# Early splits of v's first units and weights, residual loads inside an issue_after block, and gathered rows added one step after their fetch

## The chip, the cores and the metric

The kernel runs on one core of one Trainium2 chip. A core has five engines with queues of their own: TensorE (PE, with its weight loads as PEld), VectorE (DVE), ScalarE (ACT), GpSimd (POOL) and SyncE (SP), which here issues most of the DMAs. The metric is device microseconds (us) of one execution; of several runs the median counts.

## The reference

One decoder layer over 256 tokens of width 2048, in float32. What matters here is its last part, the PEER layer, and the two layer norms around it:

```python
h = layer_norm(ALPHA * x + mix, ln1_g, ln1_b)
y = layer_norm(ALPHA * h + peer_ffn(h), ln2_g, ln2_b)

def peer_ffn(xc):                      # 256 tokens, 8 heads, 16 experts a head
    ...                                # two top-16 searches give expert (16384) and gate
    u_sel = u[expert]; v_sel = v[expert]
    act = gelu(einsum('td,thkd->thk', xc, u_sel))
    return einsum('thk,thkd->td', gate * act, v_sel)
```

Each token uses 128 of the 16384 experts. An expert is a pair of rows, one of `u` and one of `v`, each of 2048 elements.

## The kernel before

**How the PEER layer is cut up.** An expert's number is `i1 * 128 + i2`. For 1408 of the 2048 columns of `u`, and for 1536 of those of `v`, the kernel doesn't gather: it runs through all 16384 experts densely, in 128 steps (one for each `i2`) of 128 experts (all `i1`). The remaining 640 columns of `u` and 512 of `v` (`GU`, `GV`) are gathered, row by row, with 256 indirect DMAs each (128 rows of a slot, for each of 128 slots and two tiles of 128 tokens).

**The stages.** After the first layer norm and the search come three stages. The *u stage* writes, for every step, the products of all tokens with 128 rows of `u` to S, a tile of 64 parts (two steps a part) in SBUF. The *extraction* (`extract`, `scatter`, 32 blocks of 8 tokens) picks each token's 128 products out of S with one-hot matrices (`at`, `bt`, `a_hot`), applies gelu and gate, and scatters the weights back into S (`aw`, `wps`). The *value stage* then runs 128 steps; a step reads its weights from S (`weights`, 128 experts by 256 tokens) and multiplies them with three units of `v` (128 by 512 each), summing in PSUM in six banks `vacc`. The last four steps run in a tail of their own from copies (`last`), followed by the residual sum, the second layer norm and the stores.

**Split float32.** A float32 operand is multiplied as two float32r halves: ScalarE casts `hi` (line 94), VectorE subtracts and gives `lo` (line 95), and each product is three matmuls, lines 119 to 121. So each step needs three `hi`, three `lo`, a `hi` and a `lo` of the weights, and 18 matmuls. There are four buffers each for `hi` and `lo`, in the pool `stream`. In the extraction the same buffers (tags `hi` and `lo`) hold `at` and `bt` of the blocks with `b % 4 < 2`; the others use four tags each of the pool `big`, alternating between even and odd blocks.

**Loads.** `load_unit` loads a unit of `v` to a `raw` tile (four buffers), or takes a part of S that has been read already and was filled ahead (`v_place`, `v_follow`, `v_unit`); 23 units, all in the first 13 steps, use `raw`, the other 361 use S. From step 13 on the plan fills 3.5 parts a step, and so runs further and further ahead of use. The loads are issued by SP.

**Gathers.** `add_gathered` takes a step's share of the 256 gathers (`spread`, steps 0 to `GVE` = 120), issues them on GpSimd (`v_gather`, line 805), and adds them with VectorE to `accg`, weighted (line 813). The buffers are three of tag `g`, and from step `LEND` on also the four of `raw`.

**Residual.** `residual` (eight calls, written behind steps 32 to 46) loads the normalized input from DRAM (`pre`) and a slice of gain and bias (`g1`, one buffer; it appears as `g<-ln`), and applies them on GpSimd (lines 827, 828).

**What sets the order.** The kernel is written with a tile framework. At compile time it puts the instructions of each engine into an order, by their place in the program, by priority (`tc.high_priority(offset=AHEAD)` moves an instruction 3000 places forward) and by its own estimate of when buffers and operands are ready; on the chip each queue then runs in that order. A tile of a tag waits until the tag's earlier tile in the same buffer has been released. `with tc.issue_after(ins)` adds an edge, of order alone, from `ins` to each instruction of the block that is on the engine of `ins`. `last_split[0]` is the VectorE instruction of the latest split. The last instructions of the extraction are copies into S by VectorE (line 748).

## Time and profile before

| | |
|---|---|
| median of 3 runs | 1747.99 us |
| the runs | 1747.92, 1747.99, 1755.24 us |
| the profiled execution's own time | 1756.99 us |
| its span, first to last instruction | 1755.2 us |
| TensorE's busy time | 1666.4 us (95%), mean granted clock 0.984 |
| VectorE | 1450.0 us (83%) |
| ScalarE, GpSimd | 897.5 us (51%), 886.7 us (51%) |
| DMA | 451.13 MB, mean 257 GB/s |

The profile is of one execution. Its lines name the engine, the line of the kernel, the operation and the tiles (`out<-in`); a bracket gives the idle time of the engine before an instruction and what ended it. Matmuls are pipelined, and a busy TensorE is not TensorE at its peak; its granted clock is given as a share of 2.4 GHz (1.00 is 2.4 GHz, 0.50 is 1.2 GHz, between them a mean over a stretch). In the trace the extraction takes from about 1011 to 1176 us, the value stage from there to about 1739 us.

### The profile page before, as it was taken

Reading aid. Unit: us, or ns where it says so; the run is one execution under the profiler, and the core shown is the slowest. Engines: PE = TensorE matmul, PEld = TensorE weight load, DVE = VectorE, ACT = ScalarE, POOL = GpSimd, SP = SyncE. Lnnn points to the kernel's source line nnn. Section 1 sums busy time; section 2 is a strip of 40 time slices with the busy share of each in tenths; the row PEclk is TensorE's granted clock in tenths of the full one; section 3 lists DMA queues with packets and bytes.
Section 4 is the critical chain, followed back from the end, with each engine's and each line's share of the span. In section 5 each row is a group of like instructions: output and inputs, shape, how many; then the busy total and the mean of one; then the engine's idle time right before and its main releaser. Section 6 shows DMA issues by size and latency. Waiting matters only on the chain. (4 is left out here: it accounts for less than half of the span.)

```text
span 1755.2 us, 33099 instructions
## 1 busy us (share of the span) xinstructions
PE 1666.4 (95%) x10652; PEld 1484.7 (85%) x10652; DVE 1450.0 (83%) x3515; ACT 897.5 (51%) x1885; POOL 886.7 (51%) x899
## 2 busy tenths in 40 slices
PE   8999999989899999999999889988999999999996
PEld 8999888869888999999999788876687888888883
DVE  6766676679999888889888798877888888889896
ACT  6545565444344555555554358773454555555551
POOL 0000000036775656566565588856747645456562
PEclk9999999989999999999999999998999999999998
DMA  7667657726688999999999841137999999999962
GB/s 219 179 188 192 203 175 261 255 79 214 193 287 268 337 361 321 323 347 336 344 330 329 293 146 55 55 103 255 296 329 333 381 338 332 338 319 328 352 200 89
DMA packets 206014, 451.13 MB, mean 257 GB/s; under 512 B 26928, under 2 KB 31472, under 8 KB 205328
## 3 DMA queue, kind: packets, MB, share of 16 engines
q1 hardware_dynamic: 164816, 297.93, 51.4%
q0 software_dynamic: 41024, 151.09, 24.7%
q8 instruction: 84, 1.38, 0.3%
q14 instruction: 90, 0.74, 0.1%
HBM read 444.59 MB, written 4.26 MB: 256 GB/s over the span
## 5 line engine op out<-in xcount | busy, mean ns | idle before, releaser
L94 ACT CAST hi<-S 128x512 fp32r<-128x512 f32 x677 | 420.4, 622 | 450.5 <-PE vacc L121 223.2
L95 DVE TENSOR_TENSOR lo<-S,hi 128x512 fp32r<-128x512 f32 x672 | 464.5, 701 | 89.6 <-ACT hi L94 81.4
L121 PE MATMUL ups<-hTh,lo 128*128 128x256 f32 x1408 | 392.2, 283 | 11.7 <-DVE lo L95 11.1
L119 PE MATMUL ups<-hTh,hi 128*128 128x256 f32 x1408 | 392.2, 280 | 4.5 <-ACT hi L94 4.2
L120 PE MATMUL ups<-hTl,hi 128*128 128x256 f32 x1408 | 394.0, 281 | 0.0
L659 POOL DMA_INDIRECT g<-u_g,e_idx x256 | 289.2, 1130 | 173.1 <-DVE g L684 119.4
L94 ACT CAST hi<-raw 128x512 fp32r<-128x512 f32 x327 | 202.0, 621 | 245.4 <-PE projT L120 58.9
L95 DVE TENSOR_TENSOR lo<-raw,hi 128x512 fp32r<-128x512 f32 x303 | 216.6, 720 | 111.3 <-ACT hi L94 107.2
L120 PE MATMUL vacc<-lo,wt 128*128 128x512 f32 x744 | 278.4, 401 | 8.6 <-DVE lo L95 8.5
L121 PEld LDWEIGHTS ups<-hTh,lo 128*128 128x128 f32 x1408 | 263.5, 189 | 16.8 <-DVE lo L95 15.6
L121 PE MATMUL vacc<-hi,wt 128*128 128x512 f32 x744 | 276.2, 399 | 0.0
L119 PEld LDWEIGHTS ups<-hTh,hi 128*128 128x128 f32 x1408 | 266.0, 189 | 6.1 <-ACT hi L94 6.1
L120 PEld LDWEIGHTS ups<-hTl,hi 128*128 128x128 f32 x1408 | 265.7, 189 | 0.0
L119 PE MATMUL vacc<-hi,wt 128*128 128x512 f32 x744 | 231.2, 400 | 7.3 <-ACT wt L94 6.9
L805 POOL DMA_INDIRECT g<-v_g,e_idx x139 | 166.3, 1196 | 128.4 <-DVE accg L813 109.0
L684 DVE SCALAR_TENSOR_TENSOR g<-g,h_gath 128x640 f32<-128x640 f32 x256 | 204.9, 820 | 16.6 <-DMA g<-u_g,e_idx 16.1
L805 POOL DMA_INDIRECT raw<-v_g,e_idx x117 | 137.2, 1173 | 84.7 <-DVE accg L813 65.2
L120 PEld LDWEIGHTS vacc<-lo,wt 128*128 128x128 f32 x744 | 141.1, 190 | 45.7 <-DVE lo L95 12.0
L119 PEld LDWEIGHTS vacc<-hi,wt 128*128 128x128 f32 x744 | 141.2, 190 | 42.9 <-ACT wt L94 8.0
L121 PEld LDWEIGHTS vacc<-hi,wt 128*128 128x128 f32 x744 | 140.9, 189 | 34.5 <-issue 0.5
L714 POOL TENSOR_SCALAR bt<-cst,slotT 128x128 f32<-128x128 f32 x192 | 126.3, 675 | 23.3 <-POOL bt L714 16.4
L294 POOL TENSOR_TENSOR bias<-bias,score 128x128 f32<-128x128 f32 (+1 forms) x16 | 11.5, 739 | 233.1 <-DMA bias<-relb 115.8
(243 smaller groups left out, 3074.1 us busy)
## 6 DMA issues: line engine op xcount, KB each, us to landing
S<-v_d SPq DMA_DIRECT2D x361, 256.0 KB, 5.1
S<-u_d SPq DMA_DIRECT2D x328, 256.0 KB, 5.3
raw<-w_t SPq DMA_DIRECT2D x100, 256.0 KB, 2.8
raw<-w_n SPq DMA_DIRECT2D x64, 256.0 KB, 2.8
raw<-w_o SPq DMA_DIRECT2D x64, 256.0 KB, 3.3
raw<-w_q SPq DMA_DIRECT2D x48, 256.0 KB, 3.1
bc<-i_dram SPq DMA_DIRECT2D x32, 256.0 KB, 3.1
raw<-u_d SPq DMA_DIRECT2D x24, 256.0 KB, 5.1
```

The costliest lines, as they stand in the source:

```text
L94: last_copy[0] = nc.scalar.copy(hi, src).ins
L95: last_split[0] = (eng or nc.vector).tensor_tensor(lo, src, hi.bitcast(F32), op=ALU.subtract).ins
L119: mm(o, l[0], r[0], start=first, stop=False)
L120: mm(o, l[0], r[1], start=False, stop=False)
L121: return mm(o, l[1], r[0], start=False, stop=last).ins
L294: nc.gpsimd.tensor_tensor(bias[:, tt, :n], bias[:, tt, :n], sel[:, tt, :n], op=ALU.add)
L659: nc.gpsimd.indirect_dma_start(out=g, out_offset=None, in_=table, in_offset=bass.IndirectOffsetOnAxis(ap=e_idx[:, tt, slot:slot + 1], axis=0))
L684: nc.vector.scalar_tensor_tensor(g, g, 1.0, h_gath[:, tt], op0=ALU.mult, op1=ALU.mult, accum_out=pd[:, tt, slot:slot + 1])
L714: eng.tensor_scalar(bt[j][:, i], iota, i2T[:, t:t + 1], None, op0=ALU.is_equal)
L805: nc.gpsimd.indirect_dma_start(out=g, out_offset=None, in_=A["v_g"], in_offset=bass.IndirectOffsetOnAxis(ap=e_idx[:, tt, slot:slot + 1], a ...
```

## The change

- `VE` = 4 units of `v` are loaded and split at block 28 of the extraction (`v_early`), the first half of the step-0 weights is split after block 16 and the second half after the last block, into two tiles `wt0` of their own; the value stage takes them from there. For that, blocks from `T // EB - VB` = 28 on keep `at` and `bt` in `big`, and the `stream` buffers are left to the units.
- The body of `residual` stands in `with tc.issue_after(last_split[0])`.
- `add_gathered` issues the gathers of its step, but adds those that were issued in the step before; one more call behind the last step takes what is left. Gathers are spread over steps `GV0` = 10 to `GVE` = 123 (before: 0 to 120), and use the `raw` buffers from step 10 on (before: 24).

```diff
--- before.py
+++ after.py
@@ -58,9 +58,12 @@
 LEAD = 5
 LAG = 1
 KEEP0 = 40
-LEND = 24
+LEND = 10
 GL = 4
-GVE = 120
+GV0 = 10
+GVE = 123
+VE = 4
+VB = 4
 ED = 2
 EA = 2
 TAIL_POOL = ((0, 1, 2), (0,))
@@ -695,7 +698,7 @@
     hot_tags = ("h5", "l5")
 
     def halves(name, tags, b, sname):
-        if b % 4 >= 2:
+        if b % 4 >= 2 or b >= T // EB - VB:
             return [big.tile([P, EB // 2, P], F32, name=name, tag=tags[b % 2 * 2 + i]) for i in range(2)]
         return [stream.tile([P, EB // 2, P], F32, name=name, tag=sname, bufs=4) for i in range(2)]
 
@@ -748,10 +751,22 @@
                 put(S[:, :, t // 2].rearrange("p a c j -> p j a c"),
                     wps[:, (i % 4 - 1) * P:(i % 4 + 1) * P].rearrange("p (j a c) -> p j a c", j=2, c=2))
 
+    def split_weights(wt, i2, sl):
+        split(paired(wt[0][:, sl]), paired(wt[1][:, sl]), step_of(i2, sl))
+
+
+    tokens = [slice(tt * P, (tt + 1) * P) for tt in range(NT)]
+    wt0 = [wqp.tile([P, T], F32R, name=f"wt0{s}", tag=f"subk{s}") for s in "hl"]
+    v_early = []
     ahead = extract(0)
     for b in range(T // EB):
         here, ahead = ahead, extract(b + 1) if b + 1 < T // EB else None
         scatter(b, *here)
+        if b == T // EB // 2:
+            split_weights(wt0, 0, tokens[0])
+        if b == T // EB - VB:
+            v_early = [load_unit(A["v_d"][n]) for n in range(VE)]
+    split_weights(wt0, 0, tokens[1])
     for tt in range(NT):
         tp = bankB("wTp")[:, :P]
         nc.tensor.transpose(tp, wT[:, tt * P:(tt + 1) * P], ident)
@@ -762,11 +777,10 @@
     acc = [[(bankA, bankB)[tt]("vacc") for c in range(NC)] for tt in range(NT)]
     accg = big.tile([P, NT, GV], F32, name="accg", tag="h1")
     nc.vector.memset(accg, 0.0)
-    def weights(i2, tts):
+    def weights(i2):
         pair = big.tile([P, 2, T], F32R, name="wt", tag=("l1", "h2")[i2 % 2])
         wt = [pair[:, n] for n in range(2)]
-        for sl in tts:
-            split(paired(wt[0][:, sl]), paired(wt[1][:, sl]), step_of(i2, sl))
+        split_weights(wt, i2, slice(0, T))
         return wt
 
     def product(wt, tt, c, w, i2):
@@ -806,10 +820,14 @@
                                      in_offset=bass.IndirectOffsetOnAxis(ap=e_idx[:, tt, slot:slot + 1], axis=0))
         return g
 
+    fetched = []
+
     def add_gathered(i2):
+
         with tc.issue_after(last_split[0]):
-            for tt, slot in spread(i2, 0, GVE):
-                g = v_gather(i2, tt, slot)
+            due = fetched[:]
+            fetched[:] = [(tt, slot, v_gather(i2, tt, slot)) for tt, slot in spread(i2, GV0, GVE)]
+            for tt, slot, g in due:
                 nc.vector.scalar_tensor_tensor(accg[:, tt], g, pd[:, tt, slot:slot + 1], accg[:, tt],
                                                op0=ALU.mult, op1=ALU.add)
 
@@ -819,26 +837,27 @@
     def residual(c, hf):
         g1 = small.tile([P, 2, T], F32, name="g1", tag="h_gath")
         sl = slice(c * 512 + hf * T, c * 512 + (hf + 1) * T)
-        for i in range(2):
-            nc.sync.dma_start(g1[:, i], A["ln1"][i:i + 1, sl].broadcast_to([P, T]))
-        for tt in range(NT):
-            o = pre[tt][c][:, hf * T:(hf + 1) * T]
-            nc.sync.dma_start(o, z_dram[tt][:, sl])
-            nc.gpsimd.tensor_tensor(o, o, g1[:, 0], op=ALU.mult)
-            nc.gpsimd.tensor_tensor(o, o, g1[:, 1], op=ALU.add)
+        with tc.issue_after(last_split[0]):
+            for i in range(2):
+                nc.sync.dma_start(g1[:, i], A["ln1"][i:i + 1, sl].broadcast_to([P, T]))
+            for tt in range(NT):
+                o = pre[tt][c][:, hf * T:(hf + 1) * T]
+                nc.sync.dma_start(o, z_dram[tt][:, sl])
+                nc.gpsimd.tensor_tensor(o, o, g1[:, 0], op=ALU.mult)
+                nc.gpsimd.tensor_tensor(o, o, g1[:, 1], op=ALU.add)
 
     def finish(tt, c, lo, hi, src):
         o = pre[tt][c][:, lo:hi]
         nc.vector.scalar_tensor_tensor(o, o, ALPHA, src, op0=ALU.mult, op1=ALU.add)
 
-    tokens = [slice(tt * P, (tt + 1) * P) for tt in range(NT)]
     count[0] = 0
     for i2 in range(P - GL):
-        wt = weights(i2, tokens if i2 == 0 else [slice(0, T)])
+        wt = weights(i2) if i2 else wt0
         units = []
         for c in range(NC):
             raw = v_unit(i2, c)
-            units.append(load_unit(A["v_d"][i2 * NC + c], raw))
+            m = i2 * NC + c
+            units.append(v_early[m] if m < VE else load_unit(A["v_d"][m], raw))
             if i2:
                 for tt in range(NT):
                     product(wt, tt, c, units[c], i2)
@@ -847,6 +866,8 @@
                 for c in range(NC):
                     product(wt, tt, c, units[c], 0)
         add_gathered(i2)
+        if i2 == P - GL - 1:
+            add_gathered(P)
         if 32 <= i2 < 48 and i2 % 2 == 0:
             residual((i2 - 32) // 4, (i2 - 32) // 2 % 2)
     last = [big.tile([P, 2, T], F32, name="last", tag="l2"), small.tile([P, 2, T], F32, name="last", tag="h_gath")]
```

## Rows read from the trace of the kernel before

**Rows 1.** Windows of 42 us, all engines: busy us (instructions), clock, DMA share, GB/s.
```profile
1176.00:1218.00 42.00, 33.48 (x126) 25.37 (x127) 28.64 (x38) 16.01 (x33) 24.39 (x26) 0.88 0.74 240
...
1386.00:1428.00 42.00, 42.00 (x182) 33.81 (x181) 35.74 (x59) 21.62 (x40) 21.52 (x20) 1.00 0.99 353
```

**Rows 2.** Windows of the value sums' matmuls alone, same columns without ACT and POOL.
```profile
1192.00:1200.00 8.00, 7.42 (x26) 5.99 (x27) 0.00 (x0) 0.78 0.76 239
1208.00:1216.00 8.00, 5.97 (x18) 4.39 (x19) 0.00 (x0) 0.79 0.79 259
1240.00:1248.00 8.00, 7.65 (x27) 6.17 (x28) 0.00 (x0) 0.79 0.85 250
1342.00:1346.00 4.00, 3.62 (x9) 2.91 (x10) 0.00 (x0) 0.57 0.99 337
1358.00:1716.20 358.20, 358.20 (x1537) 288.38 (x1536) 0.00 (x0) 1.00 0.93 322
```

**Rows 3.** Timeline of TensorE, 1172 to 1350 us: start, length, [idle before <-releaser].
```profile
1192.58 1.22 PE L119 MATMUL vacc<-hi,wt 128*128 128x512 f32 x2 [5.87 <-ACT wt L94]
...
1212.03 0.50 PE L120 MATMUL vacc<-lo,wt 128*128 128x512 f32 x1 [2.03 <-DVE lo L95]
...
1240.35 0.80 PE L120 MATMUL vacc<-lo,wt 128*128 128x512 f32 x1 [3.14 <-DVE lo L95]
...
1342.38 0.79 PE L120 MATMUL vacc<-lo,wt 128*128 128x512 f32 x1 [2.52 <-DVE lo L95]
```

**Rows 4.** Timeline of VectorE, 1176 to 1250 us.
```profile
1237.08 2.62 DVE L813 SCALAR_TENSOR_TENSOR accg<-g,pd,accg 128x512 f32<-128x512 f32 x1 [3.12 <-DMA g<-v_g,e_idx]
```

**Rows 5.** Timeline of ScalarE and of SP's queue, 1176 to 1250 us.
```profile
1191.59 0.62 ACT L94 CAST hi<-raw 128x512 fp32r<-128x512 f32 x1 [7.68 <-DMA raw<-v_d]
...
1184.60 0.81 SPq L823 DMA_DIRECT2D g<-ln  x2
...
1185.51 8.36 SPq L104 DMA_DIRECT2D raw<-v_d  x5
```

**Rows 6.** Timeline of GpSimd, 1020 to 1250 us.
```profile
1130.77 1.12 POOL L805 DMA_INDIRECT g<-v_g,e_idx  x1 [0.15 <-issue]
...
1183.51 1.06 POOL L828 TENSOR_TENSOR pre<-pre,g 128x256 f32<-128x256 f32 x1
```

**Rows 7.** Timeline of GpSimd, TensorE and VectorE in the extraction.
```profile
1108.31 3.76 POOL L714 TENSOR_SCALAR bt<-cst,slotT 128x128 f32<-128x128 f32 x6 [0.83 <-POOL bt L714]
...
1112.00 1.05 PE L745 MATMUL wps<-bt,aw 128*128 128x128 f32 x8
...
1173.39 0.75 DVE L813 SCALAR_TENSOR_TENSOR accg<-g,pd,accg 128x512 f32<-128x512 f32 x1 [0.23 <-ACT pd L758]
```

**Rows 8.** Groups by form, 1176 to 1260, then 1400 to 1700 us (mean ns).
```profile
L813 DVE SCALAR_TENSOR_TENSOR accg<-g,pd,accg 128x512 f32<-128x512 f32 x22 | 21.7, 992 | 11.1 <-DMA g<-v_g,e_idx 11.1
...
L95 DVE TENSOR_TENSOR lo<-S,hi 128x512 fp32r<-128x512 f32 x26 | 22.8, 900 | 1.4 <-ACT hi L94 1.4
...
L813 DVE SCALAR_TENSOR_TENSOR accg<-raw,pd,accg 128x512 f32<-128x512 f32 x83 | 61.4, 744 | 0.0
...
L95 DVE TENSOR_TENSOR lo<-S,hi 128x512 fp32r<-128x512 f32 x214 | 146.7, 689 | 41.1 <-ACT hi L94 37.9 <-DMA S<-v_d 1.7
```

**Rows 9.** Windows of line 813, the additions, on VectorE.
```profile
1386.00:1428.00 42.00, 14.13 (x19) 1.00 0.99 353
...
1680.00:1722.00 42.00, 21.70 (x30) 1.00 0.55 157
```

**Rows 10.** Timeline of GpSimd and VectorE, late in the value stage.
```profile
1334.90 0.95 POOL L805 DMA_INDIRECT g<-v_g,e_idx  x1 [0.30 <-issue]
...
1722.62 0.73 DVE L813 SCALAR_TENSOR_TENSOR accg<-raw,pd,accg 128x512 f32<-128x512 f32 x1
...
1740.48 0.26 DVE L434 BATCH_NORM_AGGREGATE mv<-stats 128x2 f32<-128x24 f32 x1
```

**Rows 11.** Window of the value stage with its highest DMA rate, all engines.
```profile
1360.00:1380.00 20.00, 20.00 (x88) 16.09 (x87) 17.77 (x31) 10.57 (x20) 15.94 (x13) 1.00 1.04 387
```

## The prediction

> **What bounds the kernel now.** I went from the windows of the value stage to TensorE's own timeline in it, then to the engines that it waited for, then back to the extraction that comes before it. From about 1358 us to the end of the step loop at 1716.2 us TensorE is the bound and nothing else: 1537 matmuls in 358.2 us, 0.2331 us each, so 18 matmuls or 4.2 us a step, at a granted clock of 1.00 (2.4 GHz) and with no idle time [rows 1, 2]. There is nothing to win there. The first 40 steps are another matter. The first ten steps' worth of time holds 126 matmuls where a settled stretch of the same length holds 182 [rows 1], and the reader sees why in four gaps of TensorE [rows 3]: 5.87 us before 1192.58 and 2.03, 3.14 and 2.52 us before 1212.03, 1240.35 and 1342.38. Behind each gap the granted clock is below 1.00 for a while: 0.78, 0.79, 0.79 and 0.57, a mean over stretches at 1.2 and at 2.4 GHz [rows 2]. Busy time by the share of clock missing gives what that costs: 7.42 x 0.22 = 1.6, 5.97 x 0.21 = 1.25, 7.65 x 0.21 = 1.6, 3.62 x 0.43 = 1.55 us.
>
> Three of the gaps have one cause. In each, VectorE stands in front of an addition of a gathered row that hasn't landed (2.08, 3.12 and 3.10 us; the middle one is shown [rows 4]), and the `lo` halves of the next units, which TensorE waits for, are queued behind it on VectorE. With the clock: 2.03 + 1.25 + 3.14 + 1.6 + 2.52 + 1.55 = 12.1 us. The first gap is a transfer: ScalarE waits 7.68 us for a raw unit [rows 5]. SP issued it at 1185.51, right behind a pair of residual loads (`g<-ln`) issued at 1184.60, which had to wait until GpSimd had finished with the first residual (its last operation starts at 1183.51 and takes 1.06 us [rows 6]). 5.87 + 1.6 = 7.5 us.
>
> **The additions.** Moved to the step after the fetch, an addition has one step, 4.2 us, more between issue and use; the waits above were 2.08 to 3.12 us, so each is covered. Before step 11 there are no additions at all, and two of the three gaps lie there or just behind, in the time with three gather buffers. From step 10 gathers have seven, as they had from step 24. I take the whole 12.1 us off. Bounds: 12.1, and 7 if one of the three only moves to another place.
>
> **The residual loads.** `issue_after` ties an instruction to the given one only if both are on the same engine. `last_split` is a VectorE instruction; `residual` issues DMAs on SP and operations on GpSimd, none on VectorE. So I read this edit as empty. The trace has the same helper at work: in `add_gathered(0)` the gather stands in the same kind of block, behind the split of step 0, and yet GpSimd issues a gather at 1130.77 us [rows 6], in the midst of the extraction, far ahead of that step's splits. The 16 `pre` loads, 16 `g1` loads and 32 GpSimd operations therefore stay where the order of SP and GpSimd put them, right behind the extraction. What changes around them: units 0 to 3 are split in the extraction, so the raw loads of units 4 to 7 leave SP before the residual loads, and no gather stands beside them on the DMA queues for ten steps. The raw load of unit 9 can still end up behind the second pair of `g1`. Bounds 0 and 7.5 us off; half, 3.7 us, is what I take.
>
> **The early units.** The four units' splits leave the last stretch of the extraction, and so do two additions (0.75 us, the first at 1173.39 [rows 7]), which now lie between the last copies into S on VectorE; together some 2.5 us of VectorE's time (two additions and two `lo` of 0.69 us [rows 8], less some overlap). Against it: the last four blocks now take their `at` and `bt` from `big` alone, so a block's `bt` must wait until the block two before has been scattered. Today GpSimd starts a block's `bt` at 1108.31 us while the matmuls that read the `bt` of two blocks earlier run until 1112.00 + 1.05 = 1113.05 [rows 7]. That is up to 4.7 us for the whole tile and 2.6 us for its first half, which ends at about 1110.9; once for blocks 28 and 29 and perhaps again for 30 and 31. Bounds: 2.5 us off, 5.4 us on. I take 1 us off, since later blocks lose waits of other queues when they start later. The split of the first half of the step-0 weights is one small instruction on ScalarE and one on VectorE, a quarter of a unit's size; both engines have free time in the middle of the extraction, and I cost it at nothing (uncovered, under 1 us by the 0.69 us of a whole `lo`).
>
> **The gathers' end.** 256 gathers now have 113 steps, not 120: 2.27 a step where it was 2.13. VectorE pays 0.74 us for each [rows 8] and is busy 35.74 of 42 us [rows 1], so the time is there. Not so clear is the pace. Between 1386 and 1554 us four stretches of 42 us, ten steps, held 19 additions each (one is shown), though rows were behind: the last is added at 1722.62 us, 23 us after its step 119 ends by 4.2 us a step. In the last stretch it was 30, when most unit loads were done (DMA share 0.55) [rows 9, 10]. If the pace is midway between 1.9 and 2.27 a step for the 104 steps until then, and 3 a step in the last 8, 217 + 24 = 241 are done by the last step; 15 are left, and GpSimd issues one in 0.95 + 0.30 = 1.25 us [rows 10]: 19 us. Now the last addition starts 6.4 us behind the loop. The span ends 39 us behind the loop, of which about 24 must follow the last addition (14.7 us from the second aggregate at 1740.48 [rows 10] to the end, some 9 for the first tile of tokens), so 15 us are hidden. 0 to 4 us on; I take 1.
>
> **The sum.** The profiled execution's own time is 1756.99 us: 1755.2 us span and 1.8 us around it. 1757.0 - 12.1 - 3.7 - 1 + 1 = 1741.2 us. The median of the runs shown is 9.0 us lower than that execution, and one of the three runs lies 7.3 us above the other two, which is about the size of the first gap with its clock. So part of the gaps is probably not in the median runs; then 1741.2 stands as it is. If the 9 us lie elsewhere, the same gain leads to 1732.2. I take 3 of the 9 off: 1738 us, 0.57% under the median.
>
> **Two rules against it.** The operations of GpSimd that belong to the residual lengthen VectorE's: an addition takes 992 ns in the mean between 1176 and 1260 us, beside them, and 744 ns without them [rows 8]. The Trainium skill (SBUF — State Buffer, SBUF: two separate sides) says that a VectorE operation with two SBUF inputs and a GpSimd operation that reads SBUF take turns on one port pair; the trace agrees. It matters if the pin does hold (the third rival). And the Trainium skill (DMA: Bandwidth & Descriptors, Specifications) puts a core's share of HBM at about 358 GB/s; this trace moves 387 GB/s between 1360 and 1380 us, and TensorE loses nothing [rows 11], so the measurement decides. By the page's figure the estimate would be a shortage: 3.5 units and 2.27 gathers a step, 256 KB each, are 1.51 MB in 4.2 us, 360 GB/s.
>
> **Rivals.** *The first gap stays whole* (0.22). SP's order stays as it is and unit 9 comes behind `g1`: 1757.0 - 12.1 = 1744.9, or 1735.9 with the other reading of the median. For it: the empty pin. Against it: the raw units before it are out of the way. *The two-deep tiles stretch the extraction* (0.10): 1741.2 + 1 + 5.4 = 1747.6. For it: the 1108.31 against 1113.05; against it: one block's latency may shrink. *The pin holds* (0.05): the first gap goes whole, and 32 GpSimd operations fall into steps 32 to 46. Between 1176 and 1260 us, beside them, an addition took 0.25 us more and a `lo` 0.21 us more [rows 8]; for 22 additions and 45 `lo` that is 15 us of VectorE's time, and in the 63 us of those steps it has 9.4 us free. 5.5 us short and 1.6 for the clock: 1741.2 - 3.8 + 7.1 = 1744.5. *Slower: the gathers come late* (0.08). At 1.9 a step all through, 215 are done and 41 left at the last step, 51 us; behind the last addition still come those 24 us. The loop would end near 1700, so 1700 + 51 + 24 + 1.8 = 1777. It gets slower by over 0.5% when more than about 25 rows are left, that is at under 2.04 a step. For it: four windows at 1.9. Against it: 30 in the last. *Better: both kinds of gap go and the 9 us lie elsewhere* (0.05): 1757 - 12.1 - 7.5 - 9 = 1728.
>
> **How the numbers follow.** The forecast (0.50) covers 1732 to 1742 us. The 8 in 10 go from 1729 (nearly all of the better case is below) to 1749 (the first two rivals and the pin are inside; the late gathers and a little more are above). 0.5%, 8.7 us, is about what the measurement can tell from no change: faster means under 1739.2. Of the forecast 0.42 lies below that, of the first rival 0.06, and the better case 0.05: 0.53. Slower is the late gathers, 0.08. The remaining 0.39 is the same.
>
> **What would show it.** In the profile after: no additions before step 11, no wait of VectorE for a gather over 1 us, and granted clock 1.00 from about step 4 on; `pre<-z_dram` on SP still right behind the extraction (else the pin holds); the gap of TensorE at unit 9 at 0 to 6 us; the last `bt` of GpSimd no later than 1160 us or so (else the tiles); the last addition within 15 us of the loop's end (else the gathers). The prediction is wrong if a new wait of over 5 us stands in the loop, or if the loop's first steps lose their matmuls to a cause not named here.

## The result: slower by 0.9%

The changed kernel takes 1767.25 us (median of 5 runs, 1765.21 to 1770.31) against 1750.62 us for the kernel before (median of 5, 1747.92 to 1755.24): a ratio of 1.0092, 95% interval 1.0072 to 1.0112. The forecast was 1738 us, with 1729 to 1749 as its range.

The profiled execution of after takes 1765.21 us, with a span of 1763.4 us where before had 1755.2. The span falls into three parts. The loop is counted from its first matmul behind the extraction's last one (a few of step 0 run earlier, between those of the extraction); it starts at 1175.22 us (before 1176.19): 1.0 us earlier. From there to the first matmul of the last four steps it is 534.9 us (before 540.2): 5.3 us less. From that matmul to the end it is 53.3 us (before 38.8): 14.5 us more. -1.0 - 5.3 + 14.5 = +8.2 us. The medians lie 16.6 us apart; the other 8.4 us are the profiled executions' places among the runs (before's is 6.4 us above its median and slower than all five of its runs, after's 2.0 below), and no pair of rows shows what they are. So the 5.3 us by which the loop got shorter may be less, or nothing, between the medians.

The same windows of 42 us of after, all engines, columns as in [rows 1]:

```profile
1176.00:1218.00 42.00, 36.10 (x145) 27.77 (x143) 19.81 (x29) 15.29 (x30) 17.60 (x22) 0.96 0.62 182
1218.00:1260.00 42.00, 37.06 (x140) 29.27 (x141) 27.85 (x47) 19.16 (x37) 25.16 (x26) 0.88 0.82 263
1386.00:1428.00 42.00, 42.00 (x182) 33.81 (x181) 35.46 (x59) 21.96 (x40) 22.70 (x20) 1.00 0.96 340
```

The first ten steps' worth of time holds 145 matmuls now instead of 126, and VectorE does 29 instructions instead of 38 (the additions don't begin before 1237.9). But the next 42 us hold only 140. The timeline of TensorE says why; columns as in [rows 3]:

```profile
1188.62 1.12 PE L122 MATMUL vacc<-hi,wt 128*128 128x512 f32 x2 [2.65 <-ACT wt L97]
...
1197.34 0.73 PE L122 MATMUL vacc<-hi,wt 128*128 128x512 f32 x2 [1.31 <-ACT hi L97]
...
1219.58 1.22 PE L122 MATMUL vacc<-hi,wt 128*128 128x512 f32 x2 [3.51 <-ACT hi L97]
...
1237.30 1.22 PE L122 MATMUL vacc<-hi,wt 128*128 128x512 f32 x2 [3.37 <-ACT hi L97]
```

There are four gaps again, but none behind VectorE: all four wait for ScalarE. ScalarE's timeline shows what it stood in front of:

```profile
1187.63 0.62 ACT L97 CAST hi<-raw 128x512 fp32r<-128x512 f32 x1 [6.14 <-DMA raw<-v_d]
...
1196.67 0.62 ACT L97 CAST hi<-raw 128x512 fp32r<-128x512 f32 x1 [6.11 <-DMA raw<-v_d]
...
1218.91 1.29 ACT L97 CAST hi<-S 128x512 fp32r<-128x512 f32 x2 [7.26 <-DMA S<-v_d]
...
1235.99 0.74 ACT L875 COPY last<-S 128x256 f32<-128x256 f32 x2 [5.38 <-POOL pre L847]
```

Three are unit loads. SP's queue shows what stands ahead of them each time (1180.76, 1188.46 and 1211.95 us), a pair of `g1` loads (`g<-ln`), which must wait for GpSimd to finish with the one `g1` buffer:

```profile
1165.58 0.81 SPq L842 DMA_DIRECT2D g<-ln  x2
1168.54 7.46 SPq L845 DMA_DIRECT2D pre<-z_dram  x13
...
1180.76 0.81 SPq L842 DMA_DIRECT2D g<-ln  x2
1181.67 2.38 SPq L107 DMA_DIRECT2D raw<-v_d  x4
1188.46 0.80 SPq L842 DMA_DIRECT2D g<-ln  x2
...
1190.25 2.75 SPq L107 DMA_DIRECT2D raw<-v_d  x4
1196.13 0.80 SPq L842 DMA_DIRECT2D g<-ln  x2
...
1211.95 0.80 SPq L842 DMA_DIRECT2D g<-ln  x2
1212.86 2.10 SPq L810 DMA_DIRECT2D S<-v_d  x4
```

The fourth is the copy `last`, which takes over the residual's buffer (tag `h_gath`) and so waits on ScalarE for the last residual operation, with `hi` casts queued behind it. And the residual is where it was, right behind the extraction: the pin is empty, as read. From 1240 us to the loop's end the waits list nothing for TensorE.

The additions, windows of their line (now 831) on VectorE as in [rows 9]:

```profile
1176.00:1218.00 42.00, 0.00 (x0) 0.96 0.62 182
1386.00:1428.00 42.00, 14.16 (x19) 1.00 0.96 340
1680.00:1722.00 42.00, 22.68 (x31) 1.00 0.58 163
1722.00:1764.00 42.00, 8.43 (x12) 0.65 0.35 112
```

The pace in the middle is the same 19 in ten steps, and it is still 31 in a late stretch; what is new is the last window, with 12 additions where before had 2. The last gather and the last addition, and what follows, in the timelines of GpSimd and VectorE (answers to [rows 10]):

```profile
1732.23 1.06 POOL L819 DMA_INDIRECT raw<-v_g,e_idx  x1 [0.30 <-issue]
...
1736.21 0.75 DVE L831 SCALAR_TENSOR_TENSOR accg<-raw,pd,accg 128x512 f32<-128x512 f32 x1 [0.76 <-DMA raw<-v_g,e_idx]
...
1745.19 0.26 DVE L437 BATCH_NORM_AGGREGATE mv<-stats 128x2 f32<-128x24 f32 x1
```

When the loop ends, 21 rows are left; the last is added 26.1 us later (before 6.2 us). Another 27.2 us come behind the start of that one: 9.0 up to the second aggregate (1745.19 us), and 18.2 from there, where before has 14.7.

### The profile page after: what moved, and what is told of

It reads as the page before. It is cut to its first block, busy times and chain, and to the rows that moved or that the text cites. A ratio compares the mean times of both kernels' runs of the same rounds, so it can differ in the third digit from the quotient of the medians.

```text
span 1763.4 us, 33129 instructions
## 1 busy us (share of the span) xinstructions
PE 1663.8 (94%) x10652; PEld 1483.7 (84%) x10652; DVE 1443.1 (82%) x3515; ACT 897.3 (51%) x1885; POOL 876.4 (50%) x899
## 5 line engine op out<-in xcount | busy, mean ns | idle before, releaser
L124 PE MATMUL ups<-hTh,lo 128*128 128x256 f32 x1408 | 391.4, 282 | 11.2 <-DVE lo L98 11.2
L124 PEld LDWEIGHTS ups<-hTh,lo 128*128 128x128 f32 x1408 | 263.7, 189 | 16.3 <-DVE lo L98 15.5
L123 PE MATMUL vacc<-lo,wt 128*128 128x512 f32 x738 | 274.6, 399 | 0.0
L124 PE MATMUL vacc<-hi,wt 128*128 128x512 f32 x738 | 273.9, 398 | 0.0
L122 PE MATMUL vacc<-hi,wt 128*128 128x512 f32 x738 | 228.0, 400 | 10.8 <-ACT hi L97 8.2
L819 POOL DMA_INDIRECT raw<-v_g,e_idx x145 | 169.6, 1170 | 118.8 <-DVE accg L831 97.4
L687 DVE SCALAR_TENSOR_TENSOR g<-g,h_gath 128x640 f32<-128x640 f32 x256 | 205.1, 821 | 18.2 <-DMA g<-u_g,e_idx 17.9
L819 POOL DMA_INDIRECT g<-v_g,e_idx x111 | 129.3, 1165 | 88.4 <-DVE accg L831 69.7
L123 PEld LDWEIGHTS vacc<-lo,wt 128*128 128x128 f32 x738 | 140.0, 190 | 34.9 <-DVE lo L98 0.9
L297 POOL TENSOR_TENSOR bias<-bias,score 128x128 f32<-128x128 f32 (+1 forms) x16 | 11.6, 746 | 233.0 <-DVE score L270 99.2
```

Of the source, the lines that this page charges most:

```text
L122: mm(o, l[0], r[0], start=first, stop=False)
L123: mm(o, l[0], r[1], start=False, stop=False)
L124: return mm(o, l[1], r[0], start=False, stop=last).ins
L297: nc.gpsimd.tensor_tensor(bias[:, tt, :n], bias[:, tt, :n], sel[:, tt, :n], op=ALU.add)
L687: nc.vector.scalar_tensor_tensor(g, g, 1.0, h_gath[:, tt], op0=ALU.mult, op1=ALU.mult, accum_out=pd[:, tt, slot:slot + 1])
L819: nc.gpsimd.indirect_dma_start(out=g, out_offset=None, in_=A["v_g"], in_offset=bass.IndirectOffsetOnAxis(ap=e_idx[:, tt, slot:slot + 1], a ...
```

## The experiments

Two theories at the start. **A, late gathers:** they begin ten steps later, keep the pace of 1.9 a step, and so the end waits for them. **C, residual on SP:** the gaps of the loop's start are unit loads behind `g1`. The numbers of all runs, loop and tail measured as above from one profile each; the ratio is against the kernel before on the same chip (its median is 1750.62 to 1766.92 us in these sets of runs, so ratios are compared, not times). "None" means that no addition is left when the loop ends:

| run | ratio, 95% interval | loop us | last addition behind loop's end, us | tail us |
|---|---|---|---|---|
| before | 1 | 540.2 | 6.2 | 38.8 |
| after | 1.0092 (1.0072 to 1.0112) | 534.9 | 26.1 | 53.3 |
| after again (e5) | 1.0098 (1.0078 to 1.0119) | 536.7 | 27.2 | 54.4 |
| e1 late gathers left out | 0.9971 (0.9957 to 0.9985) | 537.4 | none | 36.8 |
| e2 gathers from step 0 | 0.9982 (0.9967 to 0.9998) | 539.5 | 7.5 | 38.8 |
| e3 added in the same step | 1.0074 (1.0047 to 1.0102) | 536.7 | 27.8 | 55.2 |
| e4 residual held back | 1.0057 (1.0039 to 1.0075) | 521.7 | 45.0 | 69.3 |
| e6 cap on loads (no effect) | 1.0094 (1.0074 to 1.0113) | 534.0 | 28.1 | 55.4 |
| e7 held back, from step 0 | 1.0016 (1.0000 to 1.0032) | 524.1 | 24.2 | 51.6 |
| e8 the same, with the cap | 1.0008 (0.9996 to 1.0021) | 521.6 | 24.5 | 52.0 |
| e9 order forced | 1.0008 (0.9994 to 1.0023) | 544.0 | 1.8 | 38.9 |
| e10 forced, from step 0 | 1.0058 (1.0036 to 1.0079) | 549.9 | none | 39.3 |
| e11 forced, held back, step 0 | 1.0011 (0.9996 to 1.0026) | 541.8 | none | 39.3 |
| e12 the same, spread | 0.9999 (0.9985 to 1.0014) | 538.9 | none | 39.3 |
| e13 before, additions alone | 0.9971 (0.9949 to 0.9993) | 534.5 | 7.5 | 38.8 |
| e14 the same, held back | 0.9999 (0.9985 to 1.0014) | 530.1 | 29.6 | 57.1 |
| e15 residual left out | 0.9925 (0.9900 to 0.9950) | 525.4 | none | 39.3 |
| e16 VectorE relieved | 1.0152 (1.0118 to 1.0186) | 565.3 | none | 39.3 |
| e17 no early units | 1.0065 (1.0041 to 1.0089) | 542.7 | 19.1 | 46.3 |
| e18 gathers from step 4 | 1.0042 (1.0025 to 1.0060) | 539.8 | 17.9 | 46.8 |

Read down the last two columns: a last addition 6 to 8 us behind the loop costs nothing (38.8), and from some 18 us on the tail is that lag plus 24 to 29 us.

**e1, late gathers left out.** The rows of steps 112 to 122 are neither gathered nor added.

```diff
+VSTOP = 112
-            fetched[:] = [... for tt, slot in spread(i2, GV0, GVE)]
+            fetched[:] = [... for tt, slot in spread(i2, GV0, GVE) if i2 < VSTOP]
```

> The changed kernel with the value gathers of steps 112 to 122, some 25 of 256, and their additions left out (so the output lacks those rows). Theory A, the gathers come late and the end waits for their additions: the last addition falls ahead of the step loop's end near 1710 us, 39 us of tail remain behind the loop as in the kernel before, and the time falls by 12 to 16 us, to about 1752. Theory B, the tail is longer for another cause (the norms, the stores, the tail's matmuls): the time falls by under 4 us.

Without the late rows the tail is 36.8 us and the kernel is faster than before. A is confirmed: the 14.5 us are theirs. The ratio falls by 0.012, some 21 us, which is more than the 12 to 16 expected; the tail explains 16.5 to 17.6 of them (53.3 and 54.4 to 36.8), the rest is open.

**e2, gathers from step 0.**

```diff
-GV0 = 10
-GVE = 123
+GV0 = 0
+GVE = 120
```

> The changed kernel with its gathers spread over steps 0 to 120 again, all else as changed. Theory A1, they are late because they start ten steps later at a pace that can't be raised: some 20 more are done by step 10, the last addition lies within 8 us of the loop's end, time 1750 to 1755. Theory A2, they are late because an addition one step later holds its buffer longer and so lowers the pace: the last addition stays 20 us or more behind the loop, time 1762 or more.

The last addition is 7.5 us behind the loop, as A1 had it, and the tail goes back to 38.8 us, but VectorE waits for rows again in the first steps (11.8 us in 7 waits; before 27.2 in 24), and the loop is no shorter than before. So the late start, which costs the tail, is what bought the quiet first steps.

**e3, additions in the step of the fetch**, as before, with the late start kept.

```diff
-            due = fetched[:]
-            fetched[:] = [(tt, slot, v_gather(i2, tt, slot)) for tt, slot in spread(i2, GV0, GVE)]
-            for tt, slot, g in due:
+            for tt, slot in spread(i2, GV0, GVE):
+                g = v_gather(i2, tt, slot)
```

> The changed kernel with each gathered row added in the step of its fetch again, gathers still over steps 10 to 123. Theory A1 (late start): the last addition stays 20 us or more behind the loop and the time stays within 5 us of 1767. Theory A2 (buffers held longer): the pace rises above 20 in ten steps, the time falls to 1755 or less. Waits of VectorE for gathers over 2 us may come back between steps 10 and 40 by either.

Within the measurement it is the changed kernel. VectorE's waits for rows in the loop come to 2.0 us:

```profile
DVE accg L830 <- DMA g<-v_g,e_idx: 1.3, 1, 1.3
DVE accg L830 <- DMA raw<-v_g,e_idx: 0.7, 1, 0.7
```

The moved additions do nothing where gathers start at step 10 with seven buffers. How much of that is the start and how much the buffers, no run separates.

**e4, residual really held back**, by an edge from SP's own latest load.

```diff
-        with tc.issue_after(last_split[0]):
+        with tc.issue_after(last_load[0]):
             for i in range(2):
                 nc.sync.dma_start(g1[:, i], ...)
```

> The changed kernel with the residual's loads queued behind the latest load of SP instead of behind a VectorE instruction, so that they do stand in steps 32 to 46. Theory C, the four gaps of TensorE between 1188 and 1238 us (2.65, 1.31, 3.51 and 3.37 us, and the slow clock behind them) come from the residual loads in front of unit loads on SP and from what waits for the residual: all four go, and the step loop ends 12 to 16 us earlier, near 1696. The total falls by less if the gathers are what ends the kernel: between 0 and 12 us. Theory D, the gaps come from the raw buffers: they stay, and the loop's end stays within 4 us of 1710.

The loop is 521.7 us, with no gap over 0.5 us until 1704 us: C is confirmed, and the residual's place at the head costs 13.2 us of after's loop. But the last addition comes 45 us behind. Between 1320 and 1470 us, beside the residual, in the groups by form, an addition takes 877 to 884 ns and a `lo` 771 ns (744 and 689 in [rows 8]), and there are 59 additions in these 36 steps. e9 shows which of the two, the longer operations or the order of the instructions, sets that pace.

```profile
L98 DVE TENSOR_TENSOR lo<-S,hi 128x512 fp32r<-128x512 f32 x107 | 80.9, 771 | 11.4 <-ACT hi L97 8.7 <-issue 2.1 <-DMA S<-v_d 0.4
L831 DVE SCALAR_TENSOR_TENSOR accg<-raw,pd,accg 128x512 f32<-128x512 f32 x34 | 29.6, 877 | 0.0
L831 DVE SCALAR_TENSOR_TENSOR accg<-g,pd,accg 128x512 f32<-128x512 f32 x25 | 22.0, 884 | 0.0
```

**e5 to e8: what sets the pace?** Theory P: unit loads that run ahead take the DMA engines. e6 is meant to cap how far they run ahead, at 16 units; e7 joins e2 and e4; e8 has all three.

```diff
+CAP = 16
-        while v_free and (n := max(ahead_n, m + LEAD)) < P * NC:
+        while v_free and (n := max(ahead_n, m + LEAD)) < min(P * NC, m + CAP):
```

> Nothing is edited: the changed kernel again, on the chip of the three runs beside it, as the yardstick for them. Both theories: ratio to the kernel before 1.007 to 1.011, last addition of a gathered row 20 to 30 us behind the step loop's end, about 19 additions in 42 us between 1345 and 1510 us.

> The changed kernel, with the loads of v's units kept from running more than 16 units (5.3 steps) ahead of their use. Theory P (the pace of 1.9 gathered rows a step is set by unit loads that run ahead at 3.5 parts a step and take the DMA engines): the pace in the middle rises to 22 or 23 additions in 42 us, the last addition stands within 15 us of the loop's end, and the time falls by 6 to 14 us against the changed kernel. Rival Q (the pace is set elsewhere: by the buffers of the gathered rows or GpSimd's queue): still 19 additions in 42 us, last addition 20 us or more behind the loop, and the time within 3 us of the changed kernel. A cap that is too short would show as new waits of ScalarE for unit loads in the loop, and as gaps of TensorE.

> The changed kernel, with the residual really held back (issue_after on SP's own latest load) and the gathers spread from step 0 to 120 as before. Theory A with C (the tail is late gathers that start ten steps late; the loop's gaps come from residual loads on SP and GpSimd): the loop has no gap over 1 us up to step 32, the last addition comes 5 to 25 us behind the loop's end instead of 45, and the ratio to the kernel before is 0.985 to 0.995. Rival: gathers from step 0 bring VectorE's waits for gathered rows back in the first steps (each over 1 us, with gaps of TensorE), or the residual operations waiting in GpSimd's queue still hold the gathers back so that the last addition is 30 us or more behind the loop; then 0.997 to 1.005.

> The same as the run before (residual held back, gathers from step 0), with unit loads also kept within 16 units of their use. Theory P with A and C: additions of 21 or more in every 42 us, last addition within 10 us of the loop's end, loop of about 521 us without gaps: ratio to the kernel before 0.983 to 0.990. Rival Q: no different from the run without the cap (within 3 us), because the pace doesn't depend on how far the loads run ahead.

The cap decides nothing, because it didn't take effect. The instructions of SP, VectorE, ScalarE and GpSimd stand in the same order in e6 as in after, and the loads leave at the same pace. Timelines of SP's queue, after and then e6:

```profile
1230.85 427.00 SPq L810 DMA_DIRECT2D S<-v_d  x346
```

```profile
1233.43 425.87 SPq L811 DMA_DIRECT2D S<-v_d  x346
```

When the 300th unit load is issued, 261 units have been cast in either run: the loads run 39 units ahead, not 16. The likely reason, which no run tests, is that they stand in a `tc.high_priority` block, which moves them forward again. So e6 is the changed kernel in effect, and neither it nor e8 tests theory P; that is left to e9. e7 and e8 have the loop that C promised (524.1, 521.6) and still a lag of 24 us: although the gathers start at step 0, only 14 to 17 additions come in each 42 us between 1344 and 1512 us, the residual's steps. The first range of each, 0.983 to 0.995 between them, is missed; the numbers of the rivals came.

**e9, the order forced.** The additions in the order of VectorE's instructions, in each ten steps (counted in the traces up to the split of the weights of steps 8, 18, ... 118, the last number behind that):

```
before     13 14 18 27 21 19 18 18 20 22 22 19 25
after       0 15 23 22 21 18 19 18 19 23 21 19 38
e4          0 15 23 21 16 15 16 15 18 23 21 19 54
e9          0 15 23 22 21 23 22 23 23 22 23 23 16
```

The traces of after and of e5 have all 3515 VectorE instructions in the same order. The 18 or 19 stand in that order, made at compile time, and so do the 38 of the last steps, and the 15 or 16 of e4 beside the residual: it is the order that spaces them, not the longer operations. Theory R: the chip only follows it. An edge puts each step's split of the weights behind all additions but those of the latest step (`adds` holds the last addition of each step):

```diff
+        behind = adds[-2] if len(adds) >= 2 else None
+        with tc.issue_after(behind) if behind else nullcontext():
+            split_weights(wt, i2, slice(0, T))
```

> The changed kernel, with an edge of order that makes each step's split of the weights on VectorE come behind the additions written up to there, all but the latest. Theory R (19 additions in ten steps is what the order written at compile time says, not what the chip can fetch): 22 or 23 additions in 42 us from 1260 us on, no wait of VectorE for a gathered row above 1.5 us, last addition within 12 us of the step loop's end instead of 26, ratio to the kernel before 0.999 to 1.004 (5 to 13 us better than the changed kernel); the four early gaps stay. Rival P (the chip can't fetch faster beside the unit loads, DMA share 0.95): VectorE waits for gathered rows, 10 us or more in the sum, TensorE has new gaps behind them, and the ratio is 1.005 or more.

R is confirmed. Two windows of the additions and VectorE's waits for rows from 1260 us on:

```profile
1439.00:1481.00 42.00, 16.52 (x23) 1.00 0.97 345
1481.00:1523.00 42.00, 15.62 (x22) 1.00 0.98 345
```

```profile
DVE accg L834 <- DMA raw<-v_g,e_idx: 0.7, 2, 0.4
```

The chip fetches 22 or 23 rows in ten steps beside the unit loads, and from 1260 us on VectorE waits 0.7 us for them in all. That speaks against theory P: the unit loads run as far ahead here as in after (25 and 38 units at the 200th and the 300th load, 26 and 39 in after). The tail is 38.9 us. 7 to 9 us of the loop pay for it (544.0 against 534.9 and 536.7): the split of the weights, on which TensorE waits, now stands behind additions, and some windows hold 173 to 177 matmuls instead of 182.

**e10 to e12, all cures together:** e10 is e9 with gathers from step 0, e11 has the residual held back too, e12 has one residual every four steps with its operations behind the latest gather.

```diff
+        if 32 <= i2 < 64 and (i2 - 32) % 4 == 0:
+            r = divmod((i2 - 32) // 4, 2)
+            g1 = residual(*r)
+        if 32 <= i2 < 64 and (i2 - 32) % 4 == 2:
+            residual_ops(*r, g1)
```

> The same edge, and the gathers spread over steps 0 to 120; the residual loads still right behind the extraction. Theory R: last addition at the loop's end or within 3 us of it, so the tail is as short as that of the run that left the late gathers out (about 37 us from the loop's end to the span's end), with early gaps of some 6 us left: ratio 0.993 to 0.997. Rival P: as in the run with the gathers from step 0 alone, 0.997 or more, with waits for gathered rows in the first steps.

> As the run before, with the residual held back by SP's own latest load as well. Theory R with C (the early gaps come from the residual's loads): no gap of TensorE over 1.5 us in the loop, loop of about 522 us, last addition at the loop's end: ratio 0.986 to 0.991, the best yet. Rival: the residual's operations, which stand in GpSimd's queue in front of gathers and wait there, now make VectorE wait for rows (5 us or more) in steps 32 to 60, since the order no longer gives way: ratio 0.993 or more.

> As the run before, but one residual every four steps (32 to 60), its operations two steps behind its loads and behind the latest gather in GpSimd's queue. Theory: GpSimd's waits for the residual's loads, 38 us in the run with the residual held back, fall under 10 us; if the run before had waits of VectorE for rows in steps 32 to 60 they are gone, and the time is up to 5 us under it; if it had none, the two are the same within 2 us.

No row is late any more (tail 39.3), but the loops are 549.9, 541.8 and 538.9 us. e10 goes to its rival: VectorE waits 15.8 us for `g` in 8 waits, up to 4.4 us each, in the first steps, and with the edge the split of the weights waits behind it. e11 misses the range of its first case, and e12 is the same as e11 within some 2 us. The 38 us named in e12's expectation were misread: 34.9 of them are one wait, before the first gather of e4, as its GpSimd timeline shows, and no residual operation blocks the queue there.

```profile
1216.18 1.03 POOL L819 DMA_INDIRECT raw<-v_g,e_idx  x1 [34.88 <-DMA S<-v_d]
```

What happens instead is seen between 1320 and 1470 us of e11, groups by form:

```profile
L98 DVE TENSOR_TENSOR lo<-S,hi 128x512 fp32r<-128x512 f32 x96 | 73.9, 795 | 17.7 <-ACT hi L97 10.4 <-issue 7.3
L834 DVE SCALAR_TENSOR_TENSOR accg<-raw,pd,accg 128x512 f32<-128x512 f32 x36 | 28.8, 808 | 0.0
L834 DVE SCALAR_TENSOR_TENSOR accg<-g,pd,accg 128x512 f32<-128x512 f32 x29 | 22.8, 792 | 0.0
L98 DVE TENSOR_TENSOR wt<-S,wt 128x256 fp32r<-128x256 f32 x31 | 18.4, 595 | 0.0
```

No wait for rows stands before these additions. VectorE's operations are longer, and only 31 steps' weights are split in a time in which TensorE could do 35.7 steps (150 / 4.2); TensorE's gaps in the stretch, up to 2.99 us, all wait for the weights' `lo`.

**e13 and e14, the additions by themselves.** e13 is the kernel before with nothing but the additions moved; e14 has the residual held back too, with e4's edit.

```diff
-            for tt, slot in spread(i2, 0, GVE):
-                g = v_gather(i2, tt, slot)
+            due = fetched[:]
+            fetched[:] = [(tt, slot, v_gather(i2, tt, slot)) for tt, slot in spread(i2, 0, GVE)]
+            for tt, slot, g in due:
```

> The kernel before, with nothing changed but the additions: each is written one step behind its fetch. If the term of the prediction for the additions is right by itself (the three gaps behind late rows, 12.1 us with their clock, go), the ratio to the kernel before is 0.992 to 0.996 and VectorE has no wait for a gathered row above 1 us. Rival: with three buffers for gathered rows in the first steps the waits for rows only move, because a fetch can't start before the addition of the third row back; then 0.997 to 1.003, with waits of 2 to 4 us left.

> The run before, with the residual held back by SP's own latest load; no early units, and the raw buffers used for gathered rows from step 24. If residual and additions account for the gaps of the first steps, the loop is 521 to 525 us long without them, but the order written at compile time has 14 to 17 additions in ten steps between steps 40 and 80, so that 37 rows are left for the last steps: last addition 25 us or more behind the loop, ratio 0.998 to 1.004. Rival: the early units are what removes the gaps, and without them a gap of 3 us or more stands in the first ten steps; then 1.004 or more.

e13 is 0.3% faster, the fastest of the complete versions, and less than the term promised. In VectorE's waits in its loop the rows are not gone:

```profile
DVE accg L816 <- DMA g<-v_g,e_idx: 30.5, 21, 3.1
```

30.5 us in 21 waits, where before had 22.6 in 22 for the same tag. TensorE's idle time behind VectorE is 8.2 us in e13's loop and 8.4 in before's, so the moved additions are not seen to give anything there; where the 0.3% come from is not shown. With three buffers a fetch can't be issued before the addition three rows back has run, so a later addition also makes the next fetch later: the wait moves, as the rival had it. e14 says the same, with 29.4 us in 23, and its loop of 530.1 is not the 521 to 525 expected.

**e15 and e16, VectorE's share.** e15 is e11 with gain and bias of the residual left out (the `g1` loads, not shown, and 32 operations of GpSimd), so its output lacks them; e16 is e12 with every sixth `lo` on GpSimd.

```diff
...
-                nc.gpsimd.tensor_tensor(o, o, g1[:, 0], op=ALU.mult)
-                nc.gpsimd.tensor_tensor(o, o, g1[:, 1], op=ALU.add)
```

```diff
-            units.append(v_early[m] if m < VE else load_unit(A["v_d"][m], raw))
+            units.append(v_early[m] if m < VE else load_unit(A["v_d"][m], raw, nc.gpsimd if m % 6 == 3 and m >= 30 else None))
```

> The run with the order forced, the residual held back and the gathers from step 0, with gain and bias of the residual left out: their loads and the 32 operations on GpSimd (the loads of the normalized input stay). If those operations are what costs the loop its time there (they stand in GpSimd's queue before gathers, and lengthen VectorE's operations beside them), no wait of VectorE for a row above 1.5 us is left in steps 32 to 60, the loop is 521 to 527 us, and the ratio is 0.986 to 0.991. Rival (VectorE's own load, 256 additions within the loop, is the bound): TensorE's small waits for VectorE stay all through the loop, and the ratio is 0.995 or more.

> The run with the order forced and one residual every four steps, with the lo half of every sixth unit from step 10 on subtracted by GpSimd (about 57 of them, 39 us of VectorE's time). If VectorE's load is the bound, the loop falls by 8 us or more and the ratio to 0.991 to 0.996. Rival (waits for rows, not load): GpSimd, which issues the gathers, gets busier by 1.4 us for each, gathers come later and the ratio is 1.000 or more.

e15's loop is 525.4 us, 16.4 less than e11's, and the same stretch shows the operations at their usual length:

```profile
L98 DVE TENSOR_TENSOR lo<-S,hi 128x512 fp32r<-128x512 f32 x106 | 70.9, 686 | 23.0 <-ACT hi L97 22.8
L834 DVE SCALAR_TENSOR_TENSOR accg<-raw,pd,accg 128x512 f32<-128x512 f32 x42 | 31.0, 744 | 0.0
...
L98 DVE TENSOR_TENSOR wt<-S,wt 128x256 fp32r<-128x256 f32 x35 | 14.6, 417 | 0.0
```

So gain and bias cost 0.86% there (1.0011 against 0.9925), as the first case had it, though the ratio is a little above its range. The run takes out the operations and the `g1` loads together; the lengths of VectorE's instructions point to the operations. Between 1386 and 1428 us, ten steps, e15's VectorE is busy for 36.65 us and has 5.3 us free. The lengthening in e11, by the means of the two runs, is 30 x 0.109 + 10 x 0.178 + 21 x 0.064 = 6.4 us in ten steps, an estimate, and more than is free. e16 goes to its rival: 57 `lo` halves (79.9 us) are on GpSimd, 47 of them between 1290 and 1720 us at 1397 ns each, TensorE waits 11.2 us for them, and beside them VectorE does 45 instructions in 36.44 us (1428 to 1470 us) where e15 does 62 in 36.65 (1386 to 1428 us). Whether a lighter VectorE would help is left open by it, since GpSimd was made to pay. Group of GpSimd's instructions, 1290 to 1720 us:

```profile
L98 POOL TENSOR_TENSOR lo<-S,hi 128x512 fp32r<-128x512 f32 x47 | 65.7, 1397 | 8.7 <-issue 4.7 <-ACT hi L97 3.4
```

**e17 and e18.** The changed kernel without early units (`VE = VB = 0`), and with gathers over steps 4 to 120.

> The changed kernel without the early units: none of v's units is split in the extraction, and the last four blocks keep their tiles in both pools as before (the early split of the step-0 weights stays). If the term of the prediction holds (1 us, the gain and the two-deep tiles cancel), the ratio to the kernel before stays at 1.007 to 1.012. Rival: the early units take raw loads out of the residual's way and so save a gap; without them a gap of 5 us or more before the raw units comes back and the ratio is 1.012 to 1.016. Rival on the other side: the two-deep tiles cost more than the units save; then 1.004 or less.

> The changed kernel with the gathers spread over steps 4 to 120. The order written at compile time leaves 30 rows for the last steps where the changed kernel leaves 38, and the kernel before 25: last addition 12 to 18 us behind the loop. If the late start alone sets the time, the ratio is 1.000 to 1.004, between the run from step 0 (0.998) and the changed kernel (1.009). Rival: the waits for gathered rows of the first steps are back in full (8 us or more) while rows are still late; then 1.004 or more.

e17 lies just under its first range and its interval meets those of the changed kernel: the early units bring nothing that can be measured, and may cost up to some 5 us. Its profile has the loop 7.8 us longer and the tail 7.0 shorter than after's, probably because rows that are added beside a longer loop are less late. e18 halves the late start and stays between e2 and the changed kernel, at the edge of both of its cases, with 15.5 us of waits for `g` in 5 waits: no start of the gathers is free.

## Why the prediction was wrong

Two steps of the prediction failed. In the loop it was the residual loads: they were priced by the one gap that the trace showed, 3.7 us off, and they cost three more. At the loop's end it was the gathers: the mechanism was named and its size was wrong, 1 us on where 14.5 came. In the profiles, after has 1765.2 us where the sum gave 1741.2. The loop came out 10.5 us longer than the terms said (15.8 off, 5.3 measured) and the tail 13.5 us longer (1 on, 14.5 measured), together 24.0. Two of the prediction's own signs said so: the last addition 26.1 us behind the loop instead of within 15, and a granted clock of 0.88 between 1218 and 1260 us instead of 1.00.

**The additions** (12.1 us off) came true in size, and TensorE has no gap behind VectorE in after. But the step "each is covered" was wrong, and the number was luck as far as it rests on it. The waits are gone in after, 1.6 us are left, but not by the later addition: e13 moves the additions alone and keeps 30.8 us of waits, and e3 leaves them where they were and has 2.0 us. What removes the waits is the prediction's second reason, that no row is fetched in the first ten steps and that seven buffers stand ready from step 10. I took an addition one step later as one step of slack, and left out that with three buffers the fetch is tied to an addition.

**The residual loads** (3.7 us off): the edit was read rightly, the pin is empty, and the first gap is 2.65 us, within its bounds. What the step missed is that six further pairs of `g1` follow the second one, between 1188.46 and 1229.01 us, in the loop's first ten steps, each behind GpSimd's work on the pair before and ahead of unit loads. SP's queue of the kernel before has such pairs too; the last two:

```profile
1230.21 0.81 SPq L823 DMA_DIRECT2D g<-ln  x2
...
1240.82 0.81 SPq L823 DMA_DIRECT2D g<-ln  x2
```

But VectorE was late in those steps for its own reason, so the list of TensorE's gaps showed one cause there. With that cause gone three gaps came up, 1.31, 3.51 and 3.37 us, and with e4 all went. Windows of the value sums' matmuls on TensorE in after, columns as in [rows 2] without the other engines:

```profile
1188.00:1196.00 8.00, 7.38 (x24) 0.79 0.75 182
1219.00:1227.00 8.00, 7.42 (x25) 0.79 0.75 212
1237.00:1245.00 8.00, 7.71 (x21) 0.60 0.60 177
```

By the prediction's own pricing, idle time and the share of clock missing, the first gap cost 2.65 + 7.38 x 0.21 = 4.2 us where it had been 7.5, so 3.3 went. The three new ones cost 8.2 + 7.42 x 0.21 + 7.71 x 0.40 = 12.8 us, which is more than the 10.5 us that the loop is short of the sum. What a wait was worth could be read only as far as the next wait under it.

**The early units** (1 us off): the loop starts 1.0 us earlier. The two-deep tiles did hold GpSimd up, by 4.83 us (a wait for `wps`); a second wait of 2.81 us has no releaser in the profile. The last `bt` came at 1165.85 us, later than the 1160 named; the extraction made it up. Groups of GpSimd's timeline there:

```profile
1150.94 3.53 POOL L717 TENSOR_SCALAR bt<-cst,slotT 128x128 f32<-128x128 f32 x6 [4.83 <-PE wps L748]
...
1161.67 3.52 POOL L717 TENSOR_SCALAR bt<-cst,slotT 128x128 f32<-128x128 f32 x6 [2.81 <-issue]
```

**The gathers' end** (1 us on) had the right mechanism and too small a size. 21 rows are left at the loop's end, not 15: 7 us. Behind the last addition come 27.2 us, not 24 (the 9 ahead of the second aggregate were right, the 14.7 behind it became 18.2), so 11.6 us are hidden and not 15: 3.4 us. And I took 1 us where my own numbers gave 4: 3 us. The rival that ends slower was this mechanism; it named 25 rows as the point from which it decides, on the ground that the loop would end 16 us earlier. With a loop only 5 us shorter, 21 were enough. Its chance, 0.08, was too small: four windows at 1.9 a step stood in the rows, the pace above it was taken from one window at the end, and "midway" had no row of its own. The order written at compile time could have been counted: it has 38 of 256 additions behind the split of the weights of step 118.

**The pin as a rival** (1744.5 if it held) named the right mechanism, longer operations of VectorE beside GpSimd's: e4 has the addition 0.13 us and the `lo` 0.08 us longer. Its sum took 22 additions for steps 32 to 46, where fifteen steps at 2.27 hold 34. And in e4 the loop doesn't stretch: the order has fewer additions in those steps (15 or 16 in ten), and the tail takes them (69.3 us). Where the order is forced it does stretch (e11: 541.8 us, 525.4 without the operations). The Trainium skill (SBUF — State Buffer, SBUF: two separate sides) says of such operations that they take turns on one port pair; the runs agree, `lo` 795 ns beside the residual in e11 and 686 without it in e15.

## What to carry to other kernels

Work with a fixed pace that is started later must be shown to end in time: count what is left when the loop ends, in the written order, and how much of the tail hides it. Before a wait is priced as gain, look for the next one behind it on the same stretch (here loads behind a single buffer), and for a buffer that ties the late transfer to the very instruction that is moved. An edge of order is worth what it ties: name the engine on both of its ends. And when an edit is meant as a limit, look in the trace whether it limits anything before its result is read.

## What was not expected of the hardware

The DMA engines carried 22 or 23 gathered rows in ten steps beside the unit loads at a share of 0.97 to 1.01 (345 to 365 GB/s over 42 us) with 0.7 us of waits of VectorE for them in all (e9); the pace of 19, with transfers at a share of 0.96, had looked like theirs and wasn't. And moving 57 `lo` halves (79.9 us there) from VectorE to GpSimd made the loop longer by 26 us (565.3 against 538.9 in e12): a half takes 1397 ns on GpSimd, 689 on VectorE, and VectorE's own `lo` took 846 ns beside them between 1320 and 1470 us, 777 in e12.
